# Score products of the attention and index heads: the second matmul moved from 64 rows to 128

## The chip, the cores and the metric

The kernel runs on one core of one Trainium2 chip. The metric is the device time of one execution in microseconds (us), as the median of several runs. Five engines work side by side, each on its own queue in a fixed order: TensorE (PE in the profile, with its weight loads listed apart as PEld), VectorE (DVE), ScalarE (ACT), GpSimd (POOL) and SyncE (SP), which issues most of the DMAs.

## What is computed

Two transformer blocks over 1024 tokens of width 1024, all in float32. The first block holds two kinds of attention, eight heads of width 64 each, and a mixture of 32 experts; the second holds a pooling and recurrence mixer and a gated feed-forward layer. The change touches the scores of the first block:

```python
def forgetting_attention(q, k, v, log_f):            # "fox": every head has its own k
        s = einsum('bqhd,bkhd->bhqk', q[:, start:end], k[:, :end]) * scale
        s = s + Ft[:, :, start:end, None] - Ft[:, :, None, :end]
        p = softmax(where(tk <= tq, s, -inf));  out = p @ v[:, :end]
def dsa_attention(q, k, v, qi, ki, wi):              # "dsa": one k for all heads
        dots = einsum('bqhd,bkd->bqhk', qi[:, start:end], ki[:, :end])   # index heads
        score = einsum('bqh,bqhk->bqk', wi, relu(dots))                  # masked; the best 256 keys per query
        s = einsum('bqhd,bqkd->bhqk', q, k[idx]) * scale;  p = softmax(s);  out = p @ v[idx]
```

## The kernel before

Every float32 product is made of parts that TensorE carries without loss: an operand x is split into hi + lo, and hi\*hi, hi\*lo and lo\*hi are summed in PSUM. In the dense products these are three matmuls with 128 rows of contraction each (`mm3`, lines 233 to 235). A head is only 64 wide, so for scores two of the three parts share one matmul: the query operand q holds q_hi in 64 partitions and q_lo in the other 64, `ka` holds k_hi in both halves, and one matmul over all 128 rows (line 611) gives q_hi k_hi + q_lo k_hi. The third part, q_hi k_lo, is a second matmul over the 64 rows in which q_hi lies (line 612), with `kb` = k_lo as the moving operand. `qk` writes both for one chunk of at most 512 keys (`key_chunks`), into one PSUM buffer.

`qk` is called in two places. **Index heads** (`iq_emit` in `projections`): for the query tiles 2 to 7 and eight heads, 80 pairs in all, between the dense products of the projections; ScalarE applies a relu (line 764) and VectorE adds the weighted result to the score (line 769). Once the last score is there, VectorE searches the 256 best keys per query (`select`). **Attention** (`probs`): 192 pairs over 16 heads; VectorE adds a bias and takes the minimum (line 1238), ScalarE takes the exponential (line 1242), GpSimd normalizes (line 1244), and `values` transposes the result on TensorE (line 1265), splits it on ScalarE and VectorE (lines 1268, 1269) and multiplies it with v (lines 1256, 1257). For a pair of fox heads `pairs` makes the operands ahead of their use: transposes of q and k (line 1140), hi on ScalarE (line 1146), lo on VectorE (line 1149), and DMAs on SP's queue that lay hi and lo into the right halves (line 1155). The k_lo of a pair is written by VectorE straight to its tile `kb`, one for both heads, since head s reads only the rows of its parity.

Weights come as 512 KB chunks. `fetch` (line 183) queues the load of a chunk into a raw buffer on SP, `split_w` makes hi and lo in split buffers (lines 76, 78, 79) and frees the raw one; `pump` runs both as far ahead as there are buffers, in the order of use. Pool `w1` serves the whole first block with 2 split and 2 raw buffers; the projections have a raw buffer more (`w1x`), the experts some 25 in all (`exp0`, `expr`, `expq`, the tiles of x). So there are 3 raw buffers in the projections and 2 in attention, gated merge and output projection (`w_out`, eight chunks).

The recording layer orders the instructions of each engine; SP's DMAs, too, are in a fixed order, and a DMA whose buffer is not free holds up those behind it.

Of the kernel before, what the change touches and what calls it, by code (L numbers as in the profile page):

```python
"""Hybrid attention (forgetting + sparse-indexed) block with a grouped mixture of
experts, followed by a pooling / gated-recurrence / gated-FFN block, on one core.

float32 products run as float32r passes: every operand is split exactly into
hi + lo, each of which float32r carries without loss, and the products
hi*hi, hi*lo and lo*hi are accumulated in float32.
"""
# [20 lines left out]
P = 128  # L28
# [20 lines left out]
class Chunk:  # L49
    """A piece of a weight matrix on its way through raw and split buffers."""  # L50
# [7 lines left out]
class Kernel:  # L58
# [7 lines left out]
    # ---------------------------------------------------------------- helpers  # L66
# [6 lines left out]
    def split(self, hi, lo, x, lo_eng=None, hi_eng=None):  # L73
        """hi + lo == x exactly, both exact in float32r."""
        if hi_eng is None:
            self.nc.scalar.activation(hi, x, AF.Copy)  # L76
        else:
            hi_eng.tensor_scalar(hi, x, 1.0, 1.0, op0=OP.mult, op1=OP.mult)  # L78
        (lo_eng or self.nc.vector).tensor_tensor(lo, x, hi.bitcast(F32), op=OP.subtract)  # L79
# [5 lines left out]
    # Instructions run in program order on each engine, so the program is written in the order in which  # L85
    # the engines are to take it: tick() advances a clock of TensorE's work as the long products are
    # written, and what a product's result is used for is written by later() a while after it.
# [12 lines left out]
    def later_steps(self, us, gen):  # L100
        """Write the steps of gen; it yields the delay to the next one."""
# [10 lines left out]
    def settle(self):  # L112
        """Write all that is due later."""
        while self.events:
            self.tick(max(self.events[0][0] - self.clk, 0))

    def until(self, done):
        """Write what is due until done()."""
        while not done():
            self.tick(max(self.events[0][0] - self.clk, 0))  # L120

    # Weight chunks are queued in the order of their use; raw loads and splits run ahead as far as
    # buffers are free.
    def add_w(self, es, name, cap, raws=0, side=None, only=None):
        """cap more split buffers and raws more raw ones while es is open, for the chunks in only."""
# [20 lines left out]
    def hold_w(self, name):  # L146
        """Put nothing more into the buffers of that pool."""
# [61 lines left out]
    def chunks_n(self, w, nk, cols, pieces=None, kc=2):  # L209
        """Chunks of kc row blocks of at most 512 columns, for dense_n."""  # L210
# [10 lines left out]
    def chunks_t(self, blocks, nk):  # L221
        """Chunks of 128 columns each, for dense_t."""
# [6 lines left out]
    def mm3(self, ps, w, x, first, last):  # L229
        """ps += w^T x with w = (hi, lo) stationary and x = (hi, lo) moving."""  # L230
# [6 lines left out]
    def dense_n_steps(self, chunks, x, emit, tiles=range(NT), ready=None):  # L237
        """Token-major product: emit(tile, psum) for x^T w over one block of at most 512 columns;
        x = (hi, lo) [128, nk, tokens], of which ready(tile) sees to one tile."""
# [22 lines left out]
    def dense_t_steps(self, chunks, x, emit, fine=8, first=0):  # L262
        """Feature-major product: emit(block, half, psum) for (w block)^T x over 512 tokens; a step is fine
        row blocks of w. The first blocks take the first half of the tokens before the second."""
# [21 lines left out]
    def rstd(self, pool, dst, ss, n):  # L286
        """dst = 1 / sqrt(ss / n + eps) by Newton steps; overwrites ss."""
# [3 lines left out]
        # with y -> (x y^2 - c) y, signs and powers of two pile up to -2^13, which 2^26 x and a negative  # L291
        # start make up for
# [12 lines left out]
    def norm_rows(self, pool, xt, gain, bias=None, eng=None):  # L305
        """gain * x / rms(x) + bias for one token tile; gain and bias as rows."""
# [11 lines left out]
    def norm_t(self, pool, xt, t, gain, bias=None, hT=None):  # L318
        """Token tile t of hT = split of gain * x / rms(x) + bias, feature-major."""
        self.to_hT(self.norm_rows(pool, xt, gain, bias), t, hT)  # L320

    def to_hT(self, xn, t, hT=None):
        """Token tile t of hT = split of xn, feature-major."""
# [10 lines left out]
    # ---------------------------------------------------------------- set-up  # L334
# [16 lines left out]
    def columns(self, pool, items, name, q=None):  # L351
        """Vectors of multiples of 128 as columns [128, n]: rows are loaded and transposed."""
# [16 lines left out]
    def row(self, pool, v, n, name, **kw):  # L369
        """The vector v on every partition."""  # L370
# [6 lines left out]
    # ---------------------------------------------------------------- modulation  # L377
    def ada_first(self, pool):
        """norm1_g * (1 + sc1) and sh1 as rows on every partition; one 512-column block per step."""
# [7 lines left out]
        for j in (2, 3, 0, 1):  # L387
# [4 lines left out]
            for q in range(4):  # L392
# [4 lines left out]
                if q == 1:  # L397
                    # on VectorE, with the bias: its partitions are summed below
# [16 lines left out]
    def ada_rest(self, room):  # L415
        """gt1, sh2, norm2_g * (1 + sc2), gt2 as rows in DRAM, through room [128, 4096]; steps with their times."""
# [40 lines left out]
    # ---------------------------------------------------------------- per-layer embedding branch  # L457
# [14 lines left out]
    def ple_product(self, pool):  # L472
        """p @ w_ple_proj, to ple_d, and the sums of the squares of its rows; one token tile per step."""
# [25 lines left out]
    # ---------------------------------------------------------------- rotary tables  # L499
    def rope_tables(self, pool, keep):  # L500
        """(cos, sin) tables for the index, query and key rows; 4 KB of pool's tag xn as temporaries."""
# [53 lines left out]
    def rope(self, pool, dst, src, tab, n, engs=None):  # L555
        """dst = rotary(src) for n rows of 64 per partition; tab = (cos, sin) [128, n, 64] or, to be
        broadcast, [128, 64]; engs for the products with sin, that with cos, and the sum."""
# [15 lines left out]
    def head_rstd(self, pool, sq, n):  # L573
        """1 / rms over each of n rows of 64 from their squares."""
# [5 lines left out]
    # ---------------------------------------------------------------- attention operands  # L580
    def make_k(self, pool, src, name):
        """src [128, NT, 64] token-major -> ([k_hi; k_hi], [k_lo; k_lo]), feature-major."""
# [12 lines left out]
    def make_v(self, v2, src):  # L595
        """src [128, NT, 64] -> [v_hi | v_lo]"""
# [9 lines left out]
    def qk(self, ps, q, ka, kb, k0, w, s=0):  # L606
        """ps[:, :w] = q . k over the keys k0 .. k0 + w; q = 128 queries with q_hi in the rows of
        parity s and q_lo in the others, ka = k_hi in both, kb = k_lo in the rows of parity s."""
        ww = max(w, 256)
        rows = slice(HD * s, HD * s + HD)  # L610
        self.nc.tensor.matmul(ps[:, :ww], q, ka[:, k0:k0 + ww], start=True, stop=False)
        self.nc.tensor.matmul(ps[:, :ww], q[rows], kb[rows, k0:k0 + ww], start=False, stop=True)

    # ---------------------------------------------------------------- first block: h1 and its projections
    def vectors(self, pool):
        """Per-channel vectors of both blocks as columns."""
# [15 lines left out]
    def start(self, es_w, keep, small):  # L632
        """h1, feature-major, with the per-layer embedding branch beside it; small: steps of the first
        product of h1."""
# [43 lines left out]
    def projections(self, gates):  # L678
# [9 lines left out]
        with ExitStack() as es:  # L688
# [4 lines left out]
            def small(then):  # L693
                # ik, iw, dk, dv and the forget logits
# [27 lines left out]
            # index queries and scores: rows with at most TOPK visible keys keep them all  # L722
# [100 lines left out]
    def dsa_keys(self, pa, pk, sm, tk):  # L823
        """Operands of the sparse heads that all heads share, and the forget sums, to DRAM."""
# [18 lines left out]
    def gates(self):  # L843
        """Gate logits of both branches, feature-major in DRAM; steps of 512 tokens."""
# [10 lines left out]
    def log1p_unit(self, dst, e, s, q):  # L855
        """log(1 + e) for 0 <= e <= 1 as 2 atanh(e / (2 + e)); s and q are room."""
# [1531 lines left out]
```

## Time and profile before

| | |
|---|---|
| median of 3 runs | 3589.48 us (3588.04 to 3591.31) |
| span of the profiled execution | 3587.0 us |
| busy: PE | 3278.7 us, 91% |
| busy: DVE, ACT, POOL | 2280.1, 1553.8, 934.1 us |
| index heads | 108 to 227 us |
| rest of the projections, with the search | 227 to 665 us |
| attention | 665 to 1000 us |
| gated merge, output projection | 1000 to 1200 us |
| experts, steady part | 1280 to 1900 us |

The profiled execution's own time is not given beside its span; span and median differ by 2.5 us. The stage boundaries are read from the first and last start of the lines concerned. A busy PE is not PE at its best: matmuls are pipelined and overlap in the record, so the distance from one start to the next tells what a matmul takes of the engine's time.

### The profile page before, as it was taken

The numbers are of one execution on the slowest core, as the hardware profiler recorded it, in microseconds if no ns is written. First come the engines' busy times: TensorE is split into PE (matmuls) and PEld (weight loads), VectorE is DVE, ScalarE is ACT, GpSimd is POOL, SyncE is SP. The second block draws the span as 40 slices with busy tenths as digits, with TensorE's granted clock in tenths as the row PEclk, the third lists the DMA queues.
The fourth block names the chain that finished last, engine by engine and source line by source line (L and its number), as shares of the span: only waits on it lengthen the run. The fifth ranks groups of instructions, "written<-read, shape, count | busy, mean of one in ns | idle before, by whom it ended". The sixth has DMA issues, their size and how long they took to land. (4 is left out here: it accounts for less than half of the span.)

```text
span 3587.0 us, 41185 instructions
## 1 busy us (share of the span) xinstructions
PE 3278.7 (91%) x14381; PEld 2573.2 (72%) x14381; DVE 2280.1 (64%) x3971; ACT 1553.8 (43%) x2356; POOL 934.1 (26%) x691
## 2 busy tenths in 40 slices
PE   6996678889999798999988999999999999999987
PEld 4664456656678677777766787888778888888866
DVE  6589987467755589999987655314463444444474
ACT  3443321466752376667756674311343222222232
POOL 3124142134400566666652121000010000000024
PEclk9998889899999899999999999999999999999999
DMA  6111156663154699999985221423341111111032
GB/s 196 33 58 62 43 160 216 162 158 97 42 185 158 233 306 318 323 321 328 326 275 195 85 72 67 160 97 125 133 144 53 47 53 48 42 53 48 24 126 79
DMA packets 349086, 506.48 MB, mean 141 GB/s; under 512 B 31628, under 2 KB 182560, under 8 KB 348876
## 3 DMA queue, kind: packets, MB, share of 16 engines
q1 hardware_dynamic: 327744, 461.58, 39.4%
q0 software_dynamic: 11440, 24.77, 2.6%
q10 hardware_dynamic: 9692, 17.48, 1.5%
q8 instruction: 114, 1.87, 0.2%
q14 instruction: 96, 0.79, 0.1%
HBM read 426.47 MB, written 76.20 MB: 140 GB/s over the span
## 5 line engine op out<-in xcount | busy, mean ns | idle before, releaser
L79 DVE TENSOR_TENSOR wl<-wr,wh 128x1024 fp32r<-128x1024 f32 (+1 forms) x443 | 750.2, 1716 | 393.9 <-ACT wh L76 391.9
L76 ACT ACTIVATE wh<-wr 128x1024 fp32r<-128x1024 f32 (+1 forms) x566 | 590.5, 1053 | 684.9 <-PE mm L234 250.6
L79 POOL TENSOR_TENSOR wl<-wr,wh 128x1024 fp32r<-128x1024 f32 x143 | 383.7, 2718 | 95.3 <-ACT wh L76 93.6
L233 PE MATMUL mm<-h3h,wh 128*128 128x512 f32 x768 | 301.6, 393 | 0.0
L235 PE MATMUL mm<-h3h,wl 128*128 128x512 f32 x768 | 301.4, 392 | 0.0
L234 PE MATMUL mm<-h3l,wh 128*128 128x512 f32 x768 | 301.4, 392 | 0.0
L233 PE MATMUL mm<-h2h,wh 128*128 128x512 f32 x576 | 226.3, 393 | 1.2 <-ACT h2h L76 1.2
L235 PE MATMUL mm<-h2h,wl 128*128 128x512 f32 x576 | 224.6, 390 | 0.0
L234 PE MATMUL mm<-h2l,wh 128*128 128x512 f32 x576 | 224.2, 389 | 0.0
L233 PE MATMUL mm<-wh,hTh 128*128 128x512 f32 (+1 forms) x368 | 152.2, 413 | 38.4 <-POOL wh L78 15.8
L2046 POOL MEMSET fu<- 128x2 f32 x24 | 2.3, 99 | 688.3 <-DVE fg L2052 683.6
L2073 DVE TENSOR_TENSOR acc<-acc,mm 128x512 f32<-128x512 f32 x176 | 119.5, 685 | 87.2 <-PE mm L235 86.9
L235 PEld LDWEIGHTS mm<-h3h,wl 128*128 128x128 f32 x768 | 144.4, 188 | 32.5 <-DVE wl L79 0.2
L234 PEld LDWEIGHTS mm<-h3l,wh 128*128 128x128 f32 x768 | 144.5, 188 | 32.3
L233 PEld LDWEIGHTS mm<-h3h,wh 128*128 128x128 f32 x768 | 144.5, 188 | 32.2
L234 PE MATMUL pb<-wl,xgh 128*128 128x512 f32 x256 | 108.7, 425 | 48.7 <-DVE wl L79 47.8
L234 PE MATMUL mm<-wl,fhh 128*128 128x512 f32 x384 | 151.5, 395 | 0.0
L235 PE MATMUL mm<-wh,fhl 128*128 128x512 f32 x384 | 151.4, 394 | 0.0
L233 PE MATMUL mm<-wh,fhh 128*128 128x512 f32 x384 | 150.4, 393 | 1.0 <-ACT wh L76 1.0
L234 PE MATMUL mm<-wl,hTh 128*128 128x512 f32 (+1 forms) x368 | 143.1, 389 | 4.7 <-POOL wl L79 4.7
L235 PE MATMUL mm<-wh,hTl 128*128 128x512 f32 (+1 forms) x368 | 142.6, 388 | 0.3 <-DVE hTl L79 0.3
L1244 POOL TENSOR_SCALAR sm<-sm,src 128x128 f32<-128x128 f32 (+7 forms) x128 | 94.6, 745 | 165.5 <-DVE src L1243 114.5
(595 smaller groups left out, 8097.0 us busy)
## 6 DMA issues: line engine op xcount, KB each, us to landing
wr<-in_exp_w SPq DMA_DIRECT2D x384, 512.0 KB
wr<-in_w_in SPq DMA_DIRECT2D x72, 512.0 KB
wr<-in_w_up SPq DMA_DIRECT2D x48, 512.0 KB
sg_d<-sg SPq DMA_DIRECT2D x64, 256.0 KB
score<-in_ada_w ACTq DMA_DIRECT2D x32, 512.0 KB
wr<-in_w_down SPq DMA_DIRECT2D x24, 512.0 KB
ar<-in_ada_w SPq DMA_DIRECT2D x16, 512.0 KB
x<-in_x SPq DMA_DIRECT2D x16, 512.0 KB
```

The costliest lines, as they stand in the source:

```text
L76: self.nc.scalar.activation(hi, x, AF.Copy)
L79: (lo_eng or self.nc.vector).tensor_tensor(lo, x, hi.bitcast(F32), op=OP.subtract)
L233: mm(ps, w[0], x[0], start=first, stop=False)
L234: mm(ps, w[0], x[1], start=False, stop=False)
L235: mm(ps, w[1], x[0], start=False, stop=last)
L1244: nc.gpsimd.tensor_scalar(sm, sm, rc[:, l:l + 1], 1.0, op0=OP.mult, op1=OP.mult)
L2046: nc.gpsimd.memset(st[c][0][:, :2], 0.0)
L2073: nc.vector.tensor_add(acc[:, t, cs], acc[:, t, cs], ps)
```

## The change

The second matmul of `qk` runs over all 128 rows like the first. For that, k_lo must lie in both halves of the partitions. The index heads and the dsa heads had it there already (`make_k` copies both operands to the upper half). For fox heads VectorE now writes k_lo to a scratch tile (`spl`, the one that q_lo uses, two buffers), and four DMAs per half of the tokens lay it into two tiles, one per head, as is done with k_hi. The product gains the part q_lo k_lo. `kb` gets four buffers instead of two (8 KB per partition more), and pool `w1` one raw buffer instead of two (4 KB less). Comments are gone, too, which moves line numbers little.

```diff
-    def qk(self, ps, q, ka, kb, k0, w, s=0):
+    def qk(self, ps, q, ka, kb, k0, w):
         ww = max(w, 256)
-        rows = slice(HD * s, HD * s + HD)
         self.nc.tensor.matmul(ps[:, :ww], q, ka[:, k0:k0 + ww], start=True, stop=False)
-        self.nc.tensor.matmul(ps[:, :ww], q[rows], kb[rows, k0:k0 + ww], start=False, stop=True)
+        self.nc.tensor.matmul(ps[:, :ww], q, kb[:, k0:k0 + ww], start=False, stop=True)
...
             if fox:
-                kas, kb, v2s = [tile("kas", 4) for _ in range(2)], tile("kb", 2), \
+                kas, kbs, v2s = [tile("kas", 4) for _ in range(2)], [tile("kb", 4) for _ in range(2)], \
                     [tile("v2", 3, (P, NT, P)) for _ in range(2)]
             elif j == 0:
-                ka, kb, v2 = tile("kas", 4), tile("kb", 2), tile("v2", 3, (P, NT, P))
+                ka, kb, v2 = tile("kas", 4), tile("kb", 4), tile("v2", 3, (P, NT, P))
...
                 if fox:
-                    hi = split_pair(trans(get()), self.gk_fox, kb[:, hs])
+                    lo = tile("spl", 2, (P, 512))
+                    hi = split_pair(trans(get()), self.gk_fox, lo)
                     yield
                     for s in range(2):
                         for x in range(2):
                             copy(kas[s][HD * x:HD * x + HD, hs], own(hi, s))
+                            copy(kbs[s][HD * x:HD * x + HD, hs], own(lo, s))
...
-        self.add_w(es, "w1", 2, 2)
+        self.add_w(es, "w1", 2, 1)
```

The order of the queues moves with it. **SP, the operands of the first fox pair, first half of the tokens** (`qs` are the query operands, `kas` and `kb` the key operands, `ld` loads of projected rows). Before:

```order
L1155 DMA qs<-spl 64x512
L1129 DMA ld<-fq_d 128x4x128
L1155 DMA kas<-sph 64x512 x4
L1129 DMA ld<-fk_d 128x4x128
L1129 DMA ld<-fv_d 128x4x128
```

Now:

```order
L1155 DMA qs<-spl 64x512
L1129 DMA ld<-fq_d 128x4x128
L1155 DMA kas<-sph 64x512
L1155 DMA kb<-spl 64x512
L1155 DMA kas<-sph 64x512
L1155 DMA kb<-spl 64x512
L1155 DMA kas<-sph 64x512
L1155 DMA kb<-spl 64x512
L1155 DMA kas<-sph 64x512
L1155 DMA kb<-spl 64x512
L1129 DMA ld<-fk_d 128x4x128
L1129 DMA ld<-fv_d 128x4x128
```

Four copies have become eight, in turn, and the loads behind them are later by four issues.

**PE, the second unit of four query tiles of the first fox head** (line 1233, now 1235, adds the causal mask). Before, each matmul of line 612 stood right behind its line 611:

```order
L611 MATMUL mm<-kas,qs 128x320
L612 MATMUL mm<-kb,qs 128x320
L1233 LDWEIGHTS identb
L1233 MATMUL mm<-cmask,identb 128x128
L611 MATMUL mm<-kas,qs 128x384
L612 MATMUL mm<-kb,qs 128x384
L611 MATMUL mm<-kas,qs 128x384
L612 MATMUL mm<-kb,qs 128x384
```

Now:

```order
L611 MATMUL mm<-kas,qs 128x320
L611 MATMUL mm<-kas,qs 128x384
L612 MATMUL mm<-kb,qs 128x384
L611 MATMUL mm<-kas,qs 128x384
L611 MATMUL mm<-kas,qs 128x448
L612 MATMUL mm<-kb,qs 128x320
L1235 LDWEIGHTS identb
L1235 MATMUL mm<-cmask,identb 128x128
```

At this place the second matmuls of the upper half of the keys have moved behind the first matmuls of later chunks; further on most pairs stand together as before.

**SP, gated merge to output projection** (`msg` are the gates, `w_out` the chunks of the output projection, `gt`, `wrt`, `brt` and `sh2r` small loads). Before:

```order
L183 DMA wr<-in_w_out 128x2x512
L1311 DMA msg<-sg_d 128x512 x4
L183 DMA wr<-in_w_out 128x2x512
L1311 DMA msg<-sg_d 128x512 x3
L183 DMA wr<-in_w_out 128x2x512 x2
L374 DMA gt_9759<-mod_d 128x1024
L183 DMA wr<-in_w_out 128x2x512
```

Now:

```order
L1313 DMA msg<-sg_d 128x512 x4
L183 DMA wr<-in_w_out 128x2x512
L1313 DMA msg<-sg_d 128x512 x3
L183 DMA wr<-in_w_out 128x2x512 x2
L374 DMA gt_9801<-mod_d 128x1024
```

The first chunk of `w_out` has moved behind a group of gates, and only three chunks are issued ahead of the small loads, where there were four; the next follows behind `sh2r`.

## Rows read from the trace of the kernel before

**Rows 1.** Windows by stage: length, busy us of each engine, PE clock, DMA share, GB/s

```profile
core 0: us, PE busy (x) PEld busy (x) DVE busy (x) ACT busy (x) POOL busy (x), PEclk, DMA share, GB/s
108.00:227.00 119.00, 118.81 (x417) 70.64 (x417) 76.61 (x134) 59.28 (x107) 11.23 (x11) 1.00 0.12 36
227.00:450.00 223.00, 157.47 (x603) 122.70 (x604) 215.47 (x667) 76.75 (x144) 69.30 (x60) 0.85 0.16 54
450.00:665.00 215.00, 177.19 (x713) 137.43 (x712) 149.31 (x359) 42.75 (x75) 60.81 (x44) 0.91 0.61 185
665.00:840.00 175.00, 160.70 (x771) 107.25 (x769) 113.73 (x364) 107.73 (x253) 61.60 (x74) 0.90 0.63 147
840.00:1000.00 160.00, 157.54 (x782) 107.04 (x782) 115.97 (x373) 113.70 (x264) 72.81 (x84) 1.00 0.25 62
...
1280.00:1900.00 620.00, 548.79 (x2420) 443.27 (x2419) 579.83 (x405) 416.64 (x461) 401.16 (x170) 0.94 0.92 314
```

**Rows 2.** Timeline of PE, index heads: start us, duration us, engine, line, operation

```profile
202.07 0.40 PE L234 MATMUL mm<-wl,hTh 128*128 128x512 f32 x1
202.30 0.39 PE L235 MATMUL mm<-wh,hTl 128*128 128x512 f32 x1
202.53 0.37 PE L611 MATMUL mm<-ika,iqa 128*128 128x448 f32 x1
202.83 0.46 PE L612 MATMUL mm<-ikb,iqa 64*128 64x448 f32 x1
203.22 0.49 PE L611 MATMUL mm<-ika,iqa 128*128 128x512 f32 x1
203.65 0.50 PE L612 MATMUL mm<-ikb,iqa 64*128 64x512 f32 x1
204.08 0.50 PE L233 MATMUL mm<-wh,hTh 128*128 128x512 f32 x1
204.41 0.40 PE L234 MATMUL mm<-wl,hTh 128*128 128x512 f32 x1
```

**Rows 3.** Timeline of PE's weight loads, same place; brackets: idle before it

```profile
202.30 0.19 PEld L611 LDWEIGHTS mm<-ika,iqa 128*128 128x128 f32 x1
202.83 0.18 PEld L612 LDWEIGHTS mm<-ikb,iqa 64*128 64x128 f32 x1 [0.33 <-issue]
```

**Rows 4.** Line 612: durations ns (min/median/max), first and last start, forms

```profile
L612 PE MATMUL mm<-kb,qs x192: 379/440/793, 665.6 to 990.0; 64*128 64x384 f32 x48, 64*128 64x512 f32 x48, 64*128 64x256 f32 x32, 64*128 64x320 f32 x32
...
L612 PE MATMUL mm<-ikb,iqa x80: 407/452/502, 108.5 to 226.9; 64*128 64x384 f32 x24, 64*128 64x512 f32 x24, 64*128 64x320 f32 x16, 64*128 64x448 f32 x16
```

**Rows 5.** Timeline of PE, attention (the same columns as Rows 2)

```profile
896.62 0.48 PE L611 MATMUL mm<-kas,qs 128*128 128x512 f32 x1
...
898.32 0.55 PE L1265 MATMUL tr<-ident,sm 128*128 128x128 f32 x3
```

**Rows 6.** Groups by form, DVE, 840 to 1000 us: busy us, mean ns

```profile
L1238 DVE CUSTOM_DVE_ANT_0 sm<-mm,kas 128x512 f32<-128x512 f32 x16 | 11.1, 691 | 14.9 <-PE mm L612 12.0 <-POOL sm L1244 1.9 <-issue 1.0
```

**Rows 7.** Index heads, lines 769 and 764, 100 to 230 us

```profile
L769 DVE SCALAR_TENSOR_TENSOR score<-rl,sm,score x70: 544/674/1085, 112.0 to 228.1; 128x384 f32<-128x384 f32 x21, 128x512 f32<-128x512 f32 x21, 128x320 f32<-128x320 f32 x14, 128x448 f32<-128x448 f32 x14
...
L764 ACT ACTIVATE rl<-mm x80: 428/513/606, 109.2 to 227.4; 128x384 f32<-128x384 f32 x24, 128x512 f32<-128x512 f32 x24, 128x320 f32<-128x320 f32 x16, 128x448 f32<-128x448 f32 x16
```

**Rows 8.** Line 1155, issues of the k_hi copies on SP, 640 to 840 us

```profile
L1155 SPq DMA_DIRECT2D kas<-sph x32: 461/588/692, 653.4 to 786.9; - x32
```

**Rows 9.** Timelines of SP and ACT, chunks of w_out: load issues and splits

```profile
1101.07 11.27 SPq L183 DMA_DIRECT2D wr<-in_w_out  x2
...
1115.19 1.06 ACT L76 ACTIVATE wh<-wr 128x1024 fp32r<-128x1024 f32 x1 [1.17 <-DMA wr<-in_w_out]
1118.73 1.06 ACT L76 ACTIVATE wh<-wr 128x1024 fp32r<-128x1024 f32 x1 [2.48 <-DMA wr<-in_w_out]
```

**Rows 10.** Waits in the projections: POOL 400 to 460 us, PE 227 to 665 us

```profile
POOL wh L78 <- DMA wr<-in_w_in: 35.4, 1, 35.4
...
PE mm L233 <- POOL wh L78: 15.8, 1, 15.8
```

More of the change, by code (lines that the diff above doesn't have):

```diff
@@ L1208, in pairs @@
                                               ap=[[0, P], [NH * P, NT], [1, P]]))
-                    out.append(dict(q=qs[s], ka=kas[s], kb=kb, v2=v2s[s], bias=[fb] * NT))
+                    out.append(dict(q=qs[s], ka=kas[s], kb=kbs[s], v2=v2s[s], bias=[fb] * NT))
                 else:
@@ L1230, in probs @@
                 ps = self.mmt()
-                self.qk(ps, u["q"][:, i * P:(i + 1) * P], u["ka"], u["kb"], k0, w, u["h"] % 2)
+                self.qk(ps, u["q"][:, i * P:(i + 1) * P], u["ka"], u["kb"], k0, w)
                 if u["fox"] and c == len(ch) - 1:
```

## The prediction

> **What bounds the kernel now.** I read the busy times stage by stage first, then the starts of single matmuls. In the index heads (108 to 227 us) PE is busy for 118.81 of 119 us, VectorE for 76.61, ScalarE for 59.28; in the second half of attention PE has 157.54 of 160, the next engine 115.97, and in the first half 160.70 of 175 [rows 1]. So PE ends these stages, and time taken from it there shortens them until another engine takes over. Between them lies the search, where VectorE is busy for 215.47 of 223 us [rows 1]; it begins with the last index score and moves with it. In the experts VectorE (579.83 of 620) and the DMAs (0.92) are the limit [rows 1]; they too only move, as long as their weights come in time.
>
> What PE does in that time is seen at the starts. In the index heads a matmul of 512 columns starts 0.23 us before its successor when both use 128 rows (lines 234, 235 at 202.07 and 202.30, then line 611 at 202.53) [rows 2]; at 2.4 GHz the granted clock of 1.00 [rows 1] makes 512 columns 0.213 us, so this is the columns and 0.02 more. Around line 612, with 64 rows, the distances are longer: line 611 with 448 columns holds the engine for 0.30 us instead of 0.21, line 612 for 0.39 instead of 0.21, the next line 611 (512 columns) for 0.43, line 612 again for 0.43, and the dense matmul behind it for 0.33 instead of 0.235 [rows 2]. The weight loads show why: that of line 611 begins at 202.30, with the matmul before it, while that of line 612 begins at 202.83, when its own matmul is recorded, after 0.33 us of idle in which nothing that the profile shows was awaited [rows 3]. A load for a changed number of rows waits until the engine is empty, and one for the same number of rows runs ahead.
>
> **The index heads.** Seven matmuls, two pairs among them, take 204.41 - 202.07 = 2.34 us. With 128 rows throughout they take (5 x 512 + 2 x 448) / 2400 = 1.44 us and 7 x 0.02, together 1.58. That is 0.76 for two pairs, 0.38 for one, and 80 pairs [rows 4] give 30 us. The other two engines keep up: per pair VectorE's addition takes a median of 0.674 us and ScalarE's relu 0.513 [rows 7], against 0.79 us per pair on PE afterwards. Both have splits and copies besides: 76.61 us of VectorE must fit into 119 - 30 = 89. I take 27; the ends are 20 and 30. The part q_lo k_lo costs nothing of its own, since a matmul's distance goes with its columns (line 611 and line 612 have the same).
>
> **Attention.** At 512 columns four matmuls of the scores take 898.32 - 896.62 = 1.70 us instead of 4 x 0.235 = 0.94 [rows 5], so again 0.38 for a pair next to another; where a pair stands alone, the load after it still costs 0.19 and the load before line 612 some 0.09, as in [rows 2]. Between 0.28 and 0.38, say 0.335, times 192 pairs [rows 4] makes 64 us of PE's time in 335.
>
> How much of that arrives is the largest open term. In 840 to 1000 us it takes PE from 157.5 to about 125, and VectorE (116.0) and ScalarE (113.7) are then nearly as long [rows 1]. One chunk of 512 keys occupies VectorE's line 1238 for 0.691 us [rows 6]. Pairs that follow one another at 0.85 us leave VectorE time; at 0.47 us they no longer do, and the step is 0.69: of 0.38 only 0.16 remain, 40%. Where transposes and value products lie between the pairs, all of it remains. Between 40% (26 us) and 100% (64) I take 58%, 37 us, nearer the lower end because three engines then have about equal loads and each waits for the others.
>
> What PE saves here costs something in preparation: per half of a fox pair four more copies on SP, 32 in all, at a median issue of 0.588 us [rows 8], 19 us of SP's time over some 130. The DMA share is 0.63 there [rows 1] and a pair has a quarter of the fox heads' time, so I take the later pairs to be ready in time. The first pair has no work ahead of it: its line 612 waits for k_lo, now by way of four copies, 2.4 us, and a landing. Bounds 0 and 6, taken 3. The scratch tile is asked for twice as often, but its two buffers are emptied by DMAs that are issued before the next transposes; nothing is taken for it.
>
> **One raw buffer less.** Where a group of chunks is needed at once, the load of the next must now wait for the split of the last one. One such step in full: a load issued at 1112.0 (the second of the two, at the end of 11.27 us) is split at 1115.19, so 3.2 us; then 1.06 on ScalarE [rows 9] and about as long on VectorE; 5.5 us. Today the fourth and fifth chunk of the output projection arrive just in time already (ScalarE waited 1.17 and 2.48 us for them) [rows 9], and SP's order now has one chunk fewer ahead of the small loads. I count one such step at the beginning of the output projection, one between its two column halves, and one in the projections, where PE already waited 15.8 us for a split by GpSimd [rows 10]: 16 us. At the other places (the start, the remaining products) VectorE's search or a chunk loaded long ahead covers it; if that cover is gone, seven steps make 39; if all is covered, 0. In attention only the last gate chunks are used, spread over 335 us, so nothing. In the experts one of some 25 buffers is gone: at 314 GB/s [rows 1] 0.5 MB less loaded ahead is 1.7 us; taken 1.
>
> **The sum.** -27 - 37 + 3 + 16 + 1 = -44 us. The profiled span of 3587.0 stands 2.5 under the median of 3589.5, and such a distance should remain: 3589.5 - 44 = 3545.
>
> **The rivals.** (a) PE stays the bound throughout: 30 + 64 less some 8 for the raw buffer: 3504. For it: in 840 to 1000 us PE hardly ever waits today. Against it: the loads of VectorE and ScalarE named above.
> (b) VectorE and ScalarE take over in attention almost at once, or PE, now with pauses, is granted its lower clock (the first half, with pauses, has 0.90 of 2.4 GHz, the second 1.00 [rows 1]): a quarter of 64, so -27 - 16 + 20 = -23, 3566. The Trainium skill, "TensorEngine Tiling (Array Packing)", PSUM Bottleneck, says for tiled arrays that a faster TensorE doesn't speed up the emptying of PSUM, which may become the limit; by that this case is the one to expect, and no row of before shows it, as VectorE still waits for line 612 there.
> (c) Slower, by the raw buffer alone: in the projections SP's queue stands behind stores and behind splits on GpSimd. Even with three raw buffers GpSimd waited 35.4 us for a load there [rows 10], with no harm, as enough was split already. With two, a chunk that had been loaded before this wait is loaded after it. If PE needs it in that time, the wait becomes PE's, and the stores behind it delay the operands of attention; twice 35 us is 70 against 64 gained, with 4 for the rest 3600. It decides from about 60 us of additional idle time on PE in 227 to 665 us. Against it: PE idles for 103 of these 438 us [rows 1] and VectorE sets the pace in half of them.
> (d) The change doesn't do what it says: loads with 128 rows behind one another in the same product wait too, and the distances stay; the copies and the buffer remain, 20 us: 3609. Against it are lines 234, 235 and 611, a load of 0.19 us each time and still 0.23 us apart [rows 2, 3]. The Trainium skill, "TensorE: Matmul & The Clock Gate", Part 3 (The mechanism), states that a weight load overlaps with matmuls in flight only when its row group differs; by that rule line 612 on all rows could not overlap either and (d) would hold. The trace disagrees for full loads.
>
> **How the numbers follow.** Forecast 0.60, (a) 0.13, (b) 0.12, (c) 0.09, (d) 0.06. The forecast's own bounds: 20 + 26 less 46 leaves nothing, 3589; 30 + 64 less 4 is 3500. The range of 3500 to 3592 leaves out (c), (d) and a little of (a). A measurement can tell about 0.2%, 7 us, from no change. Faster by more: nearly all of the forecast, (a) and (b), 0.83; within: 0.06; slower: 0.11.
>
> **What would show it.** In the trace of after, line 612 has 128 rows, is 0.235 us from its successor at 512 columns, and its weight load starts before it; the index heads take some 92 us instead of 119; in attention PE's waits for ScalarE and VectorE grow from almost nothing. Chunks that come late show as waits of PE for splits (lines 76 to 79) at the beginning of the output projection. I am wrong if the distances at line 612 stay, if the search doesn't begin earlier, or if PE's idle time before attention grows by tens of us.

## The result, and the profile after

The changed kernel takes 3556.7 us (median of 4 runs, 3556.4 to 3557.4) against 3588.8 (4 runs, 3580.4 to 3591.3) for the kernel before: a ratio of 0.9913, 95% interval 0.9899 to 0.9928, 32 us less. The forecast was 3545 with a range of 3500 to 3592. Its profiled span is 3555.7 us.

Windows of the changed kernel by stage (the columns of [rows 1]): index heads, search and projections in two parts, the two halves of attention.

```profile
core 0: us, PE busy (x) PEld busy (x) DVE busy (x) ACT busy (x) POOL busy (x), PEclk, DMA share, GB/s
102.00:192.00 90.00, 88.54 (x416) 74.11 (x417) 72.62 (x132) 57.50 (x107) 9.90 (x10) 1.00 0.16 48
192.00:420.00 228.00, 156.78 (x586) 121.24 (x585) 217.47 (x672) 80.49 (x152) 68.93 (x60) 0.83 0.18 59
420.00:634.00 214.00, 183.02 (x731) 142.99 (x732) 145.82 (x355) 39.01 (x68) 61.85 (x45) 0.91 0.61 181
634.00:790.00 156.00, 121.40 (x664) 96.04 (x663) 99.87 (x315) 94.81 (x223) 51.29 (x63) 0.87 0.69 166
790.00:940.00 150.00, 140.46 (x864) 117.44 (x862) 125.92 (x418) 121.53 (x288) 81.82 (x95) 1.00 0.34 85
```

The index heads take 90 us instead of 119 with nearly the same work on the other engines (72.62 us on VectorE). In attention PE, which was busy for 160.70 of 175 and 157.54 of 160 us [rows 1], now has 121.40 of 156 and 140.46 of 150: it waits in the first half.

PE in the index heads of the changed kernel, the stretch that answers to [rows 2] (start us, duration us):

```profile
179.34 0.39 PE L235 MATMUL mm<-wh,hTl 128*128 128x512 f32 x1
179.57 0.36 PE L611 MATMUL mm<-ika,iqa 128*128 128x448 f32 x1
179.77 0.37 PE L612 MATMUL mm<-ikb,iqa 128*128 128x448 f32 x1
179.97 0.39 PE L611 MATMUL mm<-ika,iqa 128*128 128x512 f32 x1
180.21 0.40 PE L612 MATMUL mm<-ikb,iqa 128*128 128x512 f32 x1
180.44 0.39 PE L233 MATMUL mm<-wh,hTh 128*128 128x512 f32 x1
180.67 0.39 PE L234 MATMUL mm<-wl,hTh 128*128 128x512 f32 x1
```

and its weight load of line 612, against [rows 3]:

```profile
179.57 0.19 PEld L612 LDWEIGHTS mm<-ikb,iqa 128*128 128x128 f32 x1
```

Starts are 0.20 us apart at 448 columns and 0.23 at 512, where they were 0.39 and 0.43 [rows 2]; the load begins with the matmul before it, with no idle ahead. The same line by count, duration and first and last start, against [rows 4]:

```profile
L612 PE MATMUL mm<-kb,qs x192: 275/340/722, 634.0 to 934.4; 128*128 128x384 f32 x48, 128*128 128x512 f32 x48, 128*128 128x256 f32 x32, 128*128 128x320 f32 x32
L612 PE MATMUL mm<-ikb,iqa x80: 303/352/398, 102.2 to 192.1; 128*128 128x384 f32 x24, 128*128 128x512 f32 x24, 128*128 128x320 f32 x16, 128*128 128x448 f32 x16
```

From such rows (first and last start of these two groups, and the span) the program falls into five stretches. Attention is cut once more at the last addition of the forget sums (`fb`), which is read by the fox pairs alone. Here for the kernel before and after and for four of the runs that follow, in us:

| | before | after | e1 one raw buffer | e2 and copies | e4 and rows in attention | e12 no copies |
|---|---|---|---|---|---|---|
| to the first index score | 108.5 | 102.2 | 101.1 | 104.7 | 101.8 | 102.2 |
| index heads | 118.4 | 89.9 | 118.4 | 118.4 | 118.6 | 89.8 |
| search, projections | 438.7 | 441.9 | 438.7 | 439.5 | 437.7 | 440.0 |
| attention | 324.4 | 300.4 | 323.0 | 333.4 | 298.6 | 283.1 |
| of it from the first `fb` on, fox | 175.9 | 175.6 | 174.5 | 184.8 | 174.4 | 159.0 |
| of it the rest, dsa | 148.0 | 124.4 | 148.0 | 148.0 | 123.8 | 123.7 |
| behind attention | 2597.0 | 2621.3 | 2626.3 | 2628.4 | 2626.1 | 2601.1 |

Three things stand in it: the index heads gave 28.5 us; attention gave 24.0, **all of it in the dsa heads**, where the change copies nothing, and none in the fox pairs; and 24.3 us were lost behind attention, where the change touches no line of code.

### The profile page after: what moved, and what is told of

Its sections match the earlier page's. It is cut to its first block, busy times and chain, and to the rows that moved or that the text cites. A ratio compares the mean times of both kernels' runs of the same rounds, so it can differ in the third digit from the quotient of the medians.

```text
span 3555.7 us, 41222 instructions
## 1 busy us (share of the span) xinstructions
PE 3207.8 (90%) x14381; PEld 2581.2 (73%) x14381; DVE 2280.0 (64%) x3971; ACT 1548.2 (44%) x2356; POOL 934.7 (26%) x691
## 5 line engine op out<-in xcount | busy, mean ns | idle before, releaser
L235 PE MATMUL mm<-h3h,wl 128*128 128x512 f32 x768 | 302.8, 394 | 5.0 <-DVE wl L79 5.0
L235 PE MATMUL mm<-h2h,wl 128*128 128x512 f32 x576 | 224.6, 390 | 0.0
L233 PE MATMUL mm<-wh,hTh 128*128 128x512 f32 (+1 forms) x368 | 146.6, 398 | 32.1 <-POOL wh L78 15.8
L235 PEld LDWEIGHTS mm<-h3h,wl 128*128 128x128 f32 x768 | 144.8, 189 | 38.8 <-DVE wl L79 6.7
L234 PE MATMUL pb<-wl,xgh 128*128 128x512 f32 x256 | 108.5, 424 | 47.9 <-DVE wl L79 46.5
L235 PE MATMUL mm<-wh,fhl 128*128 128x512 f32 x384 | 151.4, 394 | 0.0
L235 PE MATMUL mm<-wh,hTl 128*128 128x512 f32 (+1 forms) x368 | 142.2, 387 | 0.0
L233 PE MATMUL mm<-hTh,wh 128*128 128x512 f32 x256 | 111.6, 436 | 33.6 <-ACT fqr L784 15.6
```

The costliest lines, as they stand in the source:

```text
L233: mm(ps, w[0], x[0], start=first, stop=False)
L234: mm(ps, w[0], x[1], start=False, stop=False)
L235: mm(ps, w[1], x[0], start=False, stop=last)
```

## Experiment 1: the change taken apart (e1 to e4)

**e1**, the kernel before with one line of the change:

```diff
-        self.add_w(es, "w1", 2, 2)
+        self.add_w(es, "w1", 2, 1)
```

> The kernel before with one raw buffer of pool w1 in place of two, nothing else. Theory R (the raw buffer is the common one of the whole program, so it costs wherever no other pool has raw buffers): of the distances between the two traces some 3 us belong to it around the output projection, 6 at the end of the experts, 10 where the second block's mix_add meets the feed-forward part, 8.5 at the end of the program; the earlier start of the index heads (6 us) belongs to it too, so 3587 + 3 + 3 + 6 + 18.5 - 6 = about 3612. Theory O (what is lost in the second block comes from something else in the change, the buffer costs only what the prediction counted, 16 + 1, before the experts): about 3606 with no loss behind 1960 us. Rival N (it is free): 3589.

Measured: 3608.2 us, ratio 1.0073 (1.0050 to 1.0096), 23 us more. The time alone doesn't decide, since it lies between theory O's 3606 and theory R's 3612; the place does. The table has 7.4 us less ahead of the index heads and 29.3 more behind attention, and behind 1960 us, where theory O has no loss, the feed-forward part takes 778.0 us in e1 instead of 768.6 (measured as in experiment 2). So theory R holds. One of the places is seen in the waits for chunks where the second block's mixer ends and the feed-forward part begins, on ScalarE and, in the line on L235, on PE; first of the kernel before (2595 to 2690 us), then of the changed one (2545 to 2650); columns: us in total, times, longest:

```profile
ACT wh L76 <- DMA wr<-in_w_up: 4.0, 2, 3.3
ACT wh L76 <- DMA wr<-in_w_o: 2.2, 3, 1.9
```

```profile
PE mm L235 <- DVE wl L79: 5.0, 4, 2.3
ACT wh L76 <- DMA wr<-in_w_o: 21.7, 7, 4.7
ACT wh L76 <- DMA wr<-in_w_up: 12.3, 4, 4.2
```

Pool `w1` is open to the end of the program, not for the first block alone. The chunks of `w_o` and, at the very end, of `w_ple_gate` have no other raw buffers than its own; with one, each load waits for the split of the chunk before it.

**e2**, the changed kernel with line 612 back on 64 rows in both places (the line numbers in this run move), so that copies and buffer are left without the gain; **e3** and **e4** have the 128 rows in the index heads alone and in attention alone:

```diff
+    def qk64(self, ps, q, ka, kb, k0, w, s=0):
+        ww = max(w, 256)
+        rows = slice(HD * s, HD * s + HD)
+        self.nc.tensor.matmul(ps[:, :ww], q, ka[:, k0:k0 + ww], start=True, stop=False)
+        self.nc.tensor.matmul(ps[:, :ww], q[rows], kb[rows, k0:k0 + ww], start=False, stop=True)
...
-                            self.qk(ps2, qa[:, h // 2, h % 2], *ik, k0, cw)
+                            self.qk64(ps2, qa[:, h // 2, h % 2], *ik, k0, cw)
```

> The changed kernel with k_lo still copied to both halves of a tile per head and one raw buffer, but both score products with line 612 on 64 rows as before: the price of copies and buffer without the gain. Theory: as e1 plus what the 32 copies cost; with PE at its old speed the forget sums (fb) of a pair land about when they are needed, so 0 to 8 us over e1. Rival (the copies alone cost the 10 us by which attention gained less than predicted): e1 + 10 or more.

> The changed kernel with line 612 on 128 rows in the index heads and on 64 rows in attention. Theory: the index heads are bound by PE alone and nothing behind them takes it back, so e2 minus 28 (30 us of distances, 27 predicted). Rival (the search or the projections take part of it back): e2 minus 20 or less.

> The changed kernel with line 612 on 128 rows in attention and on 64 rows in the index heads. Theory F (the first half of attention is held up at each new fox pair by the load of the forget sums, which stands on SP's queue behind the new copies; waits of 6 us at three pairs): e2 minus 25 to 30, with those three waits on VectorE. Theory V (VectorE and ScalarE take over, as in the prediction's 58%): e2 minus 37, the waits being spread. The two gains together should give the changed kernel: e2 - 28 - (e2 - e4) = 3557.

Measured: e2 3626.5 us (1.0119, 1.0102 to 1.0136), 18 over e1; e3 3596.9 (1.0036, 1.0022 to 1.0051), 30 under e2; e4 3583.5 (0.9994, 0.9983 to 1.0004), 43 under e2. With e1's 23 the four make 23 + 18 - 30 - 43 = -32, what the whole change measured: the parts add. The index heads are as the theory had them. The copies are not: the rival held (10 us or more). In the table they cost 10.3 us in the fox pairs (174.5 to 184.8; e3, whose fox pairs are those of e2, has 185.3) and nothing in the dsa heads (148.0 both); some 3.6 us of the 18 lies ahead of the first index score, where the two programs are alike. For e4 neither number was right (43 against 25 to 30 and 37), though the waits that theory F names are there; in the trace attention itself is 34.8 us shorter than in e2, and the other 7 us lie outside it. The rows of `fb` in e2 and in the changed kernel (sat idle until, us, times):

```profile
  DMA fb<-f_d: 14.4, 3
```

```profile
  DMA fb<-f_d: 20.1, 4
```

and one of them on VectorE in the changed kernel:

```profile
689.13 0.29 DVE L1240 CUSTOM_DVE_ANT_0 sm<-mm,fb 128x128 f32<-128x128 f32 x1 [5.95 <-DMA fb<-f_d]
```

In the kernel before it was 4.0 us in all. The rows of 128 gave 10.4 us in the fox pairs (184.8 to 174.4) and 24.2 in the dsa heads; the copies took the 10.3 back.

## Experiment 2: an edit against each of the two losses (e5 to e7)

**e5** issues the first `fb` load of a pair earlier; `load_fb` holds the lines that issued it:

```diff
                 yield
+                if fox and half:
+                    fbs = [load_fb(2 * j)]
                 for s in range(2):
                     copy(own(qs[s], s)[:, hs], own(hi, s))
...
-                    fb = tile("fb", 2, dt=F32)
...
+                    fb = fbs[0] if s == 0 else load_fb(2 * j + 1)
```

> The changed kernel, the load of the forget sums for the first head of a fox pair issued before the copies of the second half of the keys instead of behind them. Theory F: the three waits of 5.7 to 6.1 us that VectorE has for it at the second, third and fourth pair (17.7 us together) go away, PE then runs into the next limit and keeps two thirds: 3557 - 12 = 3545, all of it between 640 and 790 us. Rival V (VectorE and ScalarE have about as much work as PE there and are the limit, the waits being only where it shows): 3557 - 3 at most. Rival S (SP now stands at that load until the buffer is free, and the copies behind it come later): 3557 or above.

**e6** takes a raw buffer again once attention has given its memory back, **e7** has both edits:

```diff
         self.settle()
         es_h.close()
+        self.add_w(es, "w1r", 0, 1)
         self.es_m = es.enter_context(ExitStack())
```

> The changed kernel with a second raw buffer taken again when attention has given its memory back, in a pool of its own, to the end of the program. Theory R: what one raw buffer less costs behind attention comes back, by the distances of e1 6 us at the end of the experts, 13 between 2560 and 2700 and 8 in the final stage, and the earlier start of the index heads stays: 3557 - 27 = 3530. Rival O (it is the sum of many small shifts that another buffer shifts anew): within 8 us of 3557.

> Both edits, e5 and e6, in one kernel. They lie in different parts of the program, so their gains should add: 3557 - 12 - 27 = 3518 by theories F and R; if only R holds 3530, if only F holds 3545.

Measured: e5 3556.3 us (0.9923, 0.9906 to 0.9940), nothing gained; e6 3530.0 (0.9849, 0.9831 to 0.9866), as expected to the microsecond; e7 3535.6 (0.9865, 0.9849 to 0.9882), no faster than e6 alone. Theory F falls: in e5 the wait for `fb` is down to 1.7 us, and ScalarE now waits, between 634 and 790 us, for the stores of the results, which stand behind on the same queue:

```profile
ACT potmp L1290 <- DMA out_dfox<-potmp: 23.1, 5, 6.7
```

That was 2.8 us in the changed kernel. So the wait for `fb` was where the loss showed, not what set it. Rivals S and V both have a kernel that gains nothing here, so e5 doesn't tell them apart; e12 speaks against V.

For theory R, the stretches behind attention by the first and last start of their matmuls on line 233 (output projection `mTh`, experts `xgh`, feed-forward part `h3h`, gate at the end `fhT`), first before, then after, then e6:

```profile
L233 PE MATMUL mm<-wh,mTh x128: 389/389/497, 1109.2 to 1217.2; 128*128 128x512 f32 x128
L233 PE MATMUL pa<-wh,xgh x256: 387/389/796, 1255.8 to 1929.9; 128*128 128x512 f32 x128
L233 PE MATMUL mm<-h3h,wh x768: 387/392/478, 2649.5 to 3418.1; 128*128 128x512 f32 x192
L233 PE MATMUL mm<-wh,fhT x128: 391/397/628, 3466.0 to 3580.7; 128*128 128x512 f32 x128
```

```profile
L233 PE MATMUL mm<-wh,mTh x128: 389/389/505, 1053.1 to 1164.2; 128*128 128x512 f32 x128
L233 PE MATMUL pa<-wh,xgh x256: 387/389/792, 1200.6 to 1879.6; 128*128 128x512 f32 x128
L233 PE MATMUL mm<-h3h,wh x768: 387/392/628, 2600.5 to 3378.4; 128*128 128x512 f32 x192
L233 PE MATMUL mm<-wh,fhT x128: 389/397/793, 3429.0 to 3549.4; 128*128 128x512 f32 x128
```

```profile
L233 PE MATMUL mm<-wh,mTh x128: 389/389/497, 1049.8 to 1157.9; 128*128 128x512 f32 x128
L233 PE MATMUL pa<-wh,xgh x256: 387/389/796, 1196.1 to 1868.8; 128*128 128x512 f32 x128
L233 PE MATMUL mm<-h3h,wh x768: 387/392/774, 2587.8 to 3358.9; 128*128 128x512 f32 x192
L233 PE MATMUL mm<-wh,fhT x128: 391/397/628, 3406.7 to 3519.2; 128*128 128x512 f32 x128
```

Last less first: 108.0, 111.1, 108.1 in the output projection; 674.1, 679.0, 672.7 in the experts; 768.6, 777.9, 771.1 in the feed-forward part; 114.7, 120.4, 112.5 at the end. The buffer's price lies in these four, and with it back all four are back. The other runs divide in the same way: with one buffer (e1 to e5, e8) the feed-forward part takes 778 us and the output projection 111 to 112, with a second one behind attention (e6, e7, e9 to e12) 770 to 771 and 108. e6 is, up to the end of the fox pairs, instruction for instruction the changed kernel, and yet its fox pairs took 169.8 us by the same measure, not 175.6: single profiles tell this stretch to some 6 us only.

## Experiment 3: what it is that costs at line 612 (e8)

```diff
-                            self.qk(ps2, qa[:, h // 2, h % 2], *ik, k0, cw)
+                            self.qk3(ps2, qa[:, h // 2, h % 2], *ik, k0, cw)
...
+        lo = slice(0, HD)
+        mm(ps[:, :ww], q[lo], ka[lo, k0:k0 + ww], start=True, stop=False)
+        mm(ps[:, :ww], q[lo], kb[lo, k0:k0 + ww], start=False, stop=False)
+        mm(ps[:, :ww], q[lo], ka[lo, k0:k0 + ww], start=False, stop=True)
```

> The changed kernel, whose index heads now take three matmuls in place of two, each on the lower 64 rows alone (q_hi k_hi, q_hi k_lo, q_hi k_hi again; the product q_lo k_hi is left out), between dense matmuls on 128 rows. It tells what it is that costs at line 612. Theory C (the change of the number of rows costs): the three follow one another at their columns' time (512 columns 0.235 us), and the two changes, into and out of 64 rows, cost about 0.38 us together, as one pair did before; with a third matmul of 0.17 us on the mean, 80 x (0.38 + 0.19) = 46 us, 3557 + 46 = 3603 at 512 columns and somewhat less at the smaller ones. Rival H (a matmul on 64 rows is slow by itself): each of the three 0.19 us more, 80 x (3 x 0.19 + 0.19) = 61, 3618.

Measured: 3596.7 us (1.0037, 1.0020 to 1.0055), 40 over the changed kernel. PE in its index heads:

```profile
190.82 0.40 PE L235 MATMUL mm<-hTh,wl 128*128 128x512 f32 x1
191.15 0.47 PE L610 MATMUL mm<-ika,iqa 64*128 64x448 f32 x1
191.46 0.36 PE L611 MATMUL mm<-ikb,iqa 64*128 64x448 f32 x1
191.66 0.36 PE L612 MATMUL mm<-ika,iqa 64*128 64x448 f32 x1
191.95 0.50 PE L233 MATMUL mm<-hTh,wh 128*128 128x512 f32 x1
192.28 0.39 PE L234 MATMUL mm<-hTl,wh 128*128 128x512 f32 x1
192.51 0.40 PE L235 MATMUL mm<-hTh,wl 128*128 128x512 f32 x1
```

Theory C. Six matmuls take 192.51 - 190.82 = 1.69 us; their columns and 0.02 each, 3 x (448 + 512) / 2400 + 0.12, are 1.32. The difference, 0.37 us, is what one pair cost before, though three matmuls with 64 rows lie between the two changes, and the middle one (191.46) is 0.20 from its successor, as with 128 rows.

## Experiment 4: why the copies cost (e9 to e12)

**e9** is e6 with the transfers at the end of a unit on other queues, **e11** is e9 with e5's edit, **e10** is e6 with half of the k_lo copies as instructions on GpSimd:

```diff
-        nc.sync.dma_start(oth[r], tmp[o])
+        nc.scalar.dma_start(oth[r], tmp[o])
...
-            nc.sync.dma_start(self.out_d["fox" if u["fox"] else "dsa"][h // 2, r, g * 512:g * 512 + 512], tmp[r])
+            nc.gpsimd.dma_start(self.out_d["fox" if u["fox"] else "dsa"][h // 2, r, g * 512:g * 512 + 512], tmp[r])
```

```diff
-                            copy(kbs[s][HD * x:HD * x + HD, hs], own(lo, s))
+                            if x != s:
+                                copy(kbs[s][HD * x:HD * x + HD, hs], own(lo, s))
+                            else:
+                                nc.gpsimd.tensor_scalar(own(kbs[s], s)[:, hs], own(lo, s).bitcast(F32), 1.0, 1.0,
+                                                        op0=OP.mult, op1=OP.mult)
```

> e6 with the two transfers that end a unit of attention taken off SP's queue: the exchange of halves (poth) is issued by ScalarE, which has just written its source, and the store of the result by GpSimd, which has just added it. e5 showed that the wait for the forget sums was not the limit itself: with it gone, ScalarE waited 23.1 us for those stores. Theory Q (the order of one queue is what the copies cost: what waits at its head holds back what stands behind it, so with these 64 off the queue the fox pairs run as in the kernel before): most of the 14 us between e1 and e2 come back in attention, 3530 - 10 = 3520. Theory T (the transfers themselves, 6.5 MB per fox pair instead of 5.5, fill the DMA engines, and whichever is last ends the pair): no gain beyond 3 us, 3527 to 3533, and the waits move to another load.

> e6 with half of the k_lo copies (those that stay on their partitions, 16 of the 32) done by GpSimd as instructions instead of transfers; 16 more instructions of 64 rows, of about 1.3 us each as its additions of that size, 21 us of its time in 156 of which it is busy 51. Theory T: half of the 14 us comes back, 3530 - 7 = 3523. Theory Q: about the same, since half of the added entries of the queue go too, so this run prices the copies and does not tell Q from T. Rival G (GpSimd's products for the softmax then come later, and the units wait for them): 3530 or above.

> e9 and e5 together. Theory Q: with the stores off SP's queue, the early load of the forget sums no longer holds them back, and the two waits are both gone: 3520 - 5 = 3515 or below. Theory T: as e7, 3530 to 3536. Rival V (VectorE and ScalarE are the limit in the first half of attention): 3530 in all three runs.

Measured: e9 3562.1 us (0.9944, 0.9927 to 0.9961), 32 slower than e6; e11 3568.2 (0.9957, 0.9941 to 0.9974); e10 3523.4 (0.9830, 0.9814 to 0.9846). e9 and e11 went a way that no theory had: in e9 GpSimd waits for the exchange of halves for more than twice the 30.5 us of e6, in the dsa heads too:

```profile
POOL potmp L1287 <- DMA poth<-potmp: 67.4, 17, 8.6
```

The next unit's result needs the tile `potmp` that this addition and the store behind it hold, so ScalarE stands there (13.8 us on that store in the fox pairs, 1.4 in e6), and PE waits 29.8 us for the hi parts that ScalarE makes behind it (line 1270), where it was 3.6 in e6. Why the exchange lands later from ScalarE's queue these runs don't tell, since two things were moved at once; so e9 speaks neither for Q nor for T. e10 has the time that T and Q expect (3523), but its interval overlaps e6's, and its fox pairs took 171.1 us against 169.8: where its 6.6 us come from the trace doesn't show. It is, with e6 beside it, the fastest kernel here that leaves the computation as it is, and both beat the kernels before and after.

**e12** is e6 without any k_lo copy: both heads of a pair share the tile that VectorE writes.

```diff
-                    lo = tile("spl", 2, (P, 512))
-                    hi = split_pair(trans(get()), self.gk_fox, lo)
+                    hi = split_pair(trans(get()), self.gk_fox, kbs[0][:, hs])
...
-                            copy(kbs[s][HD * x:HD * x + HD, hs], own(lo, s))
```

> e6 without any k_lo copy in attention: VectorE writes k_lo of both heads of a pair into one tile, as in the kernel before, and line 612 takes all 128 rows of it, so that the rows of the other head are multiplied with q_lo (this changes a part of the scores by a product of two low parts, and is there to take the time of the copies away). e9 and e10 left open whether the fox pairs are slow for the copies or for the other engines. Theory K (the 32 copies, on SP's queue and in the DMA engines, cost what they cost at 64 rows, 14 us between e1 and e2): 3530 - 14 = 3516, with the waits for the forget sums back at 4 us or less and the gain between 630 and 800 us. Rival V (in the fox pairs VectorE and ScalarE would take over anyway, the copies' price is hidden behind them): 3524 to 3530.

Measured: 3516.4 us (0.9809, 0.9793 to 0.9826), 13.6 under e6: theory K, to the microsecond. The table has it in the fox pairs (159.0 us; e6 169.8, after 175.6) and nowhere else. That is more than profiles differ: the four kernels with the same fox pairs (after, e4, e6, e8) have 169.8 to 175.6. The part on `fb` missed: VectorE still waits 10.2 us for it. Either cause brings this wait up by itself, the copies with PE at its old pace (1.6 us in e1, 14.4 in e2) and a faster PE without copies (10.2). That the copies cost is shown; by what stays open. It may be SP's order, or the DMA engines' time (share 0.69 in that stretch, 0.63 before [rows 1]). It may also be PE's order, which moves with the copies: in the fox pairs a first matmul of `qk` is followed by something other than its second in 17 to 19 places where there are copies (e2, after, e6), and in 10 or 11 where there are none (before, e1, e12). Waits for a scratch tile to be emptied, which the prediction put at nothing, are not the common cause: ScalarE has 10.5 us of them in e6, but none in the changed kernel and in e2, which pay as well.

## Why the prediction was right, and where not

- **The mechanism** held: 0.23 us from start to start, the load ahead of its matmul, and (d) falls by the changed kernel's own rows. e8 adds that it is the change of rows that costs, not the 64 rows. The sentence cited with (d) (the Trainium skill, "TensorE: Matmul & The Clock Gate", Part 3, The mechanism: a load overlaps with matmuls in flight only when its row group differs) does not agree with these traces: full loads overlap with full matmuls, 0.23 us apart with loads of 0.19.
- **Index heads**, -27 (20 to 30): 28.5 in the trace, 30 by e3.
- **Attention**, -37, or 58% of 64: e4 took 34.8 off attention's length in e2, 54%; without copies (e12 against e1) 39.9, 62%. The size was right, but as the mean of two unlike halves, and in that there is luck: of the 32 us that each half's 96 pairs hold at 0.335, the dsa heads gave 24.2 (75%) and the fox pairs 10.4 (a third), 15.5 without copies. In the dsa heads PE is still busy for 94% of the time at full clock, VectorE for 84% (125.92 of 150), and neither (a) nor (b) took place there; of the limit that the Trainium skill names for (b) ("TensorEngine Tiling (Array Packing)", PSUM Bottleneck) these rows show nothing there. In the fox pairs no engine is full (121.40 and 99.87 us of 156 on PE and VectorE), so full engines are not what holds them; the granted clock of this stretch is 0.87, where it was 0.90 [rows 1], and what that costs no run measured.
- **Copies**, +3 (0 to 6) for the first pair and nothing for the later ones: the step that failed most. They cost 10 us in the fox pairs, 14 to 18 by whole runs. The prediction counted 19 us of SP's time in some 130 and took the later pairs to be ready. It didn't ask what stands behind the copies on that queue: the load of the forget sums, needed at the first score of a pair, and the stores that free `potmp`. e5 shows that moving one of them forward makes the other late; that this order is what the 10 us are paid for is not shown.
- **Raw buffer**, +16 and +1: e1 has 23. The sign and the kind were right, the places wrong. For the two steps of 5.5 us at the output projection ScalarE's waits grew by 13.2 us, near the 11 named; here the kernel before and after:

```profile
ACT wh L76 <- DMA wr<-in_w_out: 6.9, 3, 3.3
```

```profile
ACT wh L76 <- DMA wr<-in_w_out: 20.1, 4, 6.4
```

  but PE waited 0.3 us for a split there, and the stretch is 3.1 us longer: enough was split already. The step in the projections (PE waits there for GpSimd's split 23.7 us instead of 15.8 [rows 10]) doesn't show in the time: with either number of buffers that stretch takes 438 to 442 us in the table. What did cost lies where "the remaining products" were taken as covered: experts 4.9, feed-forward part 9.3, the gate at the end 5.7. The text read `w1` as a pool of the first block; the code enters it on the stack that both blocks share.
- **Not counted at all**: 6.3 us gained ahead of the index heads. With one buffer fewer, SP issues three chunks instead of six ahead of the next rows of x, which the first products need. Before, then after:

```profile
36.27 5.53 SPq L183 DMA_DIRECT2D wr<-in_w_in  x6
41.85 2.51 SPq L647 DMA_DIRECT2D x<-in_x  x5
```

```profile
34.84 1.58 SPq L183 DMA_DIRECT2D wr<-in_w_in  x3
36.46 2.72 SPq L647 DMA_DIRECT2D x<-in_x  x3
```

The sum was -44, measured -32. By runs the gains were 30 and 43 instead of 27 and 37, the losses 18 and 23 instead of 3 and 17; two misses on either side cancel in part. Part of this stands on both sides: some 6.5 us of e2 lie outside attention and count once in the 18 and once in the 43, and in attention alone the copies cost 10.4 and the rows gave 34.8. (c), slower by the raw buffer, had the right cause and the wrong place: PE's idle time in the projections, 103 of 438 us before [rows 1], is 102 of 442 after, and the whole price, 23 us, is far from the 70 it needs.

## What to carry to other kernels

Before a buffer is given up, list every product of the whole program that has no other buffer, down to the last one, and look there for the wait; a buffer that is short of room in one stage can be given back for the others (26.7 us here by whole runs, 23.3 behind attention in the traces). For a step that adds entries to an in-order queue, ask what stands behind them and when that is needed: by the queue's spare time alone the copies of the later pairs were free here, and 10 us were paid. And between matmuls that PE takes back to back, keep the number of rows: a pair is charged for the two changes.

## What the runs showed of the hardware

- A stretch of matmuls on 64 rows between matmuls on 128 costs some 0.37 us once, alike with one in it and with three (e8: three, 0.37 us; before: one, 0.38 [rows 2]); in e8's the starts inside are 0.20 us apart at 448 columns, as with 128 rows, from the second matmul on.
- Two loads of the same size, 512 KB, land after very different times: two chunks of `w_out` 3.2 us [rows 9] and 4.9 us after their issue, the forget sums of a head, in the stretch with a DMA share of 0.69, 9.7 us after it. The second kind also writes one row to all 128 partitions; which of the two makes it late these runs don't tell. Its issue in the changed kernel, against VectorE's start at 689.13 above:

```profile
679.41 0.50 SPq L1208 DMA_DIRECT2D fb<-f_d  x1
```
- That TensorE carries the parts hi and lo without loss is what the kernel's own text says; no run here measures it.
